# Low parts of projection and down weights, and the HGRN level products, moved from GpSimd to VectorE

## The chip, the cores and the metric

One Trainium2 chip, one core of it. The metric is device microseconds (us) of one execution of the whole program; a kernel's time is the median over runs. The engines go by the profile's names: PE is TensorE's matmul, PEld its weight load, DVE is VectorE, ACT is ScalarE, POOL is GpSimd, SP is SyncE, whose queue issues nearly all DMAs.

## What is computed

One layer (DEPTH = 1) of a hybrid streaming encoder on 1,152 tokens: 128 sample tokens (8 streams of 16) and 1,024 prompt tokens, D_MODEL = 1024, everything in float32.

```python
h = rmsnorm(x, norm1_w)
proj = einsum("btd,de->bte", h, w_in)                 # 3080 columns
xa, ga, z, xbc, dt, q, fpre, ig, og = split(proj, SPLIT_IDX)
ya = rglru(causal_conv(xa)) * gelu(ga)                # Griffin RG-LRU, 256 wide
yb = ssd_mixer(z, causal_conv(xbc), dt)               # Mamba-2 SSD, 512 wide
yc = hgrn_mixer(q, fpre, ig, og)                      # HGRN2, 256 wide
x = x + concat([ya, yb, yc]) @ w_out
h2 = rmsnorm(x, norm2_w)
x = x + (silu(h2 @ w_ffn_gate) * (h2 @ w_ffn_up)) @ w_ffn_down    # D_FF = 2816
y = rmsnorm(x, final_norm_w)

def hgrn_chunk(s, (q, lf, k, v)):                     # the part that the change touches
    bc = cumsum(lf, axis=1)
    decay = exp(where(causal, bc[:, :, None] - bc[:, None], -inf))
    att = einsum("bthk,bshk,btshk->bths", q, k, decay)
    o = einsum("bths,bshv->bthv", att, v) + einsum("bthk,bhkv->bthv", q * exp(bc), s)
```

The states of the three mixers are returned too.

## The kernel before

**High and low parts.** Matmuls of the projections and of the feed-forward part run three times each (`mm3`, lines 144 to 146): high by high, high by low and low by high part. A high part is the float32 value rounded to the engine's `fp32r` form, written by ScalarE with a Copy; the low part is the value less its high part, one `tensor_tensor` subtraction with both inputs in SBUF. `load_w` (line 152) does this for a weight tile of 128 x 1024: DMA into `wr_*`, Copy into `wh_*` (line 160), subtraction into `wl_*` (line 164). `split` (line 178) does the same for any tile (lines 179 and 180). Which engine subtracts is written out: in `load_w` every fourth weight tile of the projections, and one tile of `w_out`, goes to VectorE, the rest to GpSimd (`WV`, `WO`, `XV`, `XO`); of the third chunk of `w_out` the odd tiles go to VectorE too (`eng`).

**Stages.** Tokens stand in three chunks of 384. In order of time: the norm of the input and the first projection tiles `f0`, `f1`, `q0` (`pmf`, `pmq`); `proj_vdt` (tiles `ptv`, drained by lines 428 and 430 into `dtr` and `vs`) and `proj_og` (`ptog`); the HGRN mixer `mix_c`, nine token tiles of 128, among the RG-LRU projections (`pmxa`, `pmga`) and the eight `xbc` tiles (`pmb`, line 332); the gate projections (`ptz`); the SSD mixer `mix_b`, nine token tiles, with `w_out` (`pw`) between; the build of the feed-forward input; gate and up weights in pairs (`pS_*`, `pA_*`), some 460 us; then the down projection: five groups of weights after a first, each in two column sets of 320 and 256 columns a half, four output tiles `mp` and seven products of a Strassen scheme in each. VectorE adds each product from PSUM into SBUF (line 1204, `ac_*<-ac_*,pd`).

**HGRN levels.** For each token tile, `mix_c` goes through seven levels (four for the sample tile), two at a time in `W`. VectorE subtracts (lines 488 and 489), ScalarE takes the exponential (line 490), then the query half of `W` is multiplied by `q` into the block layout `qbd`, one instruction for each half of the partitions (line 498: half 0 on VectorE, half 1 on GpSimd), and the key half by `kk` in place (line 502, GpSimd). PE multiplies `W` by `qbd` into `pat` (line 139), and VectorE copies the masked result into `attc` (line 505).

**Down weights.** `prep_a` splits a tile of two rows of blocks: `split` of the first three quarters (768 wide; `mp` 3 on GpSimd, the others on VectorE), four combinations on VectorE (lines 1107 to 1110), `split` of all four combined blocks (1024 wide, line 1111, GpSimd). The result is `as`, and PE reads it one group later.

**What sets the order.** The tile framework puts instructions into each engine's queue in an order that it works out when the program is built, from priorities (program order, with raised priority inside `feed()` and around `mix_b`) and from its own timing of every instruction on its engine. The queues are then fixed: each engine runs its own in order and waits where an input is not there. So when an instruction changes engine, the order on all engines can change.

Of the kernel before, what the change touches and what calls it, by code (L numbers as in the profile page):

```python
# [16 lines left out]
ALU = mybir.AluOpType  # L17
# [34 lines left out]
WV = 4  # L52
# [12 lines left out]
WO = 0  # L65
XV = 100
XO = 1
# [23 lines left out]
def hybrid_step(ctx, tc, xT, xTp, vec, rows, nrow, wch, wtk0, wtk1, wout, wgate, wup, wdown,  # L91
# [59 lines left out]
    wcount, pcount, bcount = [0, 0], [0, 0], [0]  # L151

    def load_w(src, n, name, raw=None, ahead=True, eng=None):
        if raw is None:
            raw = wp.tile([P, 1056], F32, tag="wraw", name=f"wr_{name}", bufs=2)
        hi = wp.tile([P, 1056], F32R, tag="whi", name=f"wh_{name}")
        lo = wp.tile([P, 1056], F32R, tag="wlo", name=f"wl_{name}")
        with feed() if ahead else nullcontext():
            dma(raw[:, 0:n], src)
            S.activation(hi[:, 0:n], raw[:, 0:n], AF.Copy)  # L160
            o = name[0] == "o"
            wcount[o] += 1
            e = V if wcount[o] % (WV, XV)[o] == (WO, XO)[o] else G
            (eng or e).tensor_tensor(lo[:, 0:n], raw[:, 0:n], hi[:, 0:n].bitcast(F32), ALU.subtract)
        return hi, lo

# [299 lines left out]
    def halves(ap, m):  # L466
        v = ap.rearrange("p j (b two m) -> p (j b) two m", two=2, m=m)
        return v[:, :, 0, :], v[:, :, 1, :]

    def mix_c(t):  # L470
# [9 lines left out]
        for lg in range(l0, NLEV, 2):  # L480
            ls = range(lg, min(lg + 2, NLEV))
            W = pr.tile([P, 2, 2, P], F32, tag="W", name=f"W{t}_{lg}", bufs=2)
            for l in ls:
                m = 64 >> l
                b0, b1 = halves(bt, m)
                w0, w1 = halves(W[:, l - lg], m)
                mid = b0[:, :, m - 1:m].to_broadcast([P, P // m, m])
                V.tensor_tensor(w1, b1, mid, ALU.subtract)
                V.tensor_tensor(w0, mid, b0, ALU.subtract)
            S.activation(W[:, 0:len(ls)], W[:, 0:len(ls)], AF.Exp)  # L490

            Q = qbd[(lg // 2) % 2]
            pa = bank("b", f"pat{t}_{lg}", [2, 2, P])
            for l in ls:
                m = 64 >> l
                for r in range(2):
                    rs = slice(r * 64, r * 64 + 64)
                    (V, G)[r].tensor_tensor(Q[rs, l - lg, :, r, :].rearrange("p j (b m) -> p j b m", m=m),  # L498
                                    W[rs, l - lg].rearrange("p j (b two m) -> p j b two m", two=2, m=m)[:, :, :, 1],
                                    q[rs].rearrange("p j (b two m) -> p j b two m", two=2, m=m)[:, :, :, 1], ALU.mult)  # L500
                w0 = halves(W[:, l - lg], m)[0]
                G.tensor_tensor(w0, w0, halves(kk, m)[0], ALU.mult)
                for j in range(2):
                    mm(pa[:, l - lg, j, :], W[:, l - lg, j, :], Q[:, l - lg, j].rearrange("p r s -> p (r s)"))
                V.copy_predicated(
                    att.rearrange("p h (b two m) -> p h b two m", two=2, m=m)[:, :, :, 1, :],
                    lev[:, l, :].rearrange("p (b m) -> p b m", m=m).unsqueeze(1).to_broadcast([P, 4, 64 // m, m]),
                    pa[:, l - lg].rearrange("p j (r b m) -> p (j r) b m", r=2, m=m))
# [590 lines left out]
    def prep_a(g, mp):  # L1099
        t = stage(1024, f"wd{g}_{mp}")  # L1100
        v = a_view(mp)
        with feed():
# [5 lines left out]
            V.tensor_tensor(t[:, :, 3], t[:, :, 0], t[:, :, 3], ALU.subtract)  # L1108
            V.tensor_tensor(t[:, :, 0], t[:, :, 2], t[:, :, 0], ALU.subtract)
            V.tensor_tensor(t[:, :, 1], t[:, :, 1], t[:, :, 0], ALU.subtract)  # L1110
            split(v[:, 0, :, 3:7], v[:, 1, :, 3:7], t, G)


    acc = {}
# [281 lines left out]
```

## Time and profile before

| | us |
|---|---|
| median of 3 runs | 1501.31 (1500.36 to 1501.39) |
| profiled execution, whole | 1499.57 |
| its span, first to last instruction | 1497.8 |
| mean granted TensorE clock | 0.96 |
| PE busy | 1367.8 (91%) |
| DVE busy | 1122.1 (75%) |
| POOL busy | 792.9 (53%) |
| ACT busy | 513.9 (34%) |

The profiled execution is 1.77 us longer than its span and 1.74 us shorter than the median. A share of busy time is an average over stages with different limits. Of 40 equal slices of the span, those of the gate and up weights have PE busy throughout; in the others PE has gaps, and VectorE is then often the engine that is waited for.

### The profile page before, as it was taken

The page shows a single profiled execution, that of the slowest core. Times are in us where ns is not written, and L with a number is a line of the kernel's source. Part 1 is how long each engine was busy: PE and PEld are TensorE (multiplying, and loading weights), DVE is VectorE, ACT ScalarE, POOL GpSimd, SP SyncE. Part 2 cuts the span into 40 slices and gives each one's busy share as a digit, 9 for nine tenths or more (in the row PEclk, how much of TensorE's full clock was granted, in tenths as well). Part 3 has the DMA queues.
Part 4 walks back from the last instruction along what each step waited for, and adds up shares of the span by engine and source line. Part 5 has one row for each costly group of instructions (what it writes and reads, how often), then busy time and mean ns, then how long its engine had stood idle before and what let it go on. Part 6 is the DMA issues. An engine that isn't in the chain of part 4 may idle for free. (4 is left out here: it accounts for less than half of the span.)

```text
span 1497.8 us, 24592 instructions
## 1 busy us (share of the span) xinstructions
PE 1367.8 (91%) x9309; PEld 1315.9 (88%) x9309; DVE 1122.1 (75%) x2028; ACT 513.9 (34%) x839; POOL 792.9 (53%) x615
## 2 busy tenths in 40 slices
PE   7979988899997889878799999999999999988886
PEld 6979887799987778878699999999999989988876
DVE  8476799888758688599646675665666768989896
ACT  6413334333344134354322222232231443322322
POOL 5336487767345555433534554544555464475553
PEclk9989999899999899988899999999999999999988
DMA  7253221432366786841413222223322262543523
GB/s 249 75 173 102 71 68 50 104 96 75 100 224 238 225 285 208 273 167 37 150 55 112 100 96 99 70 84 113 112 98 99 85 218 85 171 149 92 172 64 127
DMA packets 103370, 193.67 MB, mean 129 GB/s; under 512 B 10380, under 2 KB 62676, under 8 KB 103124
## 3 DMA queue, kind: packets, MB, share of 16 engines
q1 hardware_dynamic: 98356, 184.24, 37.4%
q0 software_dynamic: 4896, 7.87, 1.9%
q8 instruction: 73, 1.20, 0.3%
q14 instruction: 45, 0.37, 0.1%
HBM read 136.83 MB, written 55.23 MB: 128 GB/s over the span
## 5 line engine op out<-in xcount | busy, mean ns | idle before, releaser
L144 PE MATMUL pd<-e,as 128*128 128x320 f32 (+1 forms) x560 | 170.2, 305 | 25.4 <-DVE ac_pt L1204 9.1
L145 PE MATMUL pd<-e,as 128*128 128x320 f32 (+1 forms) x560 | 166.4, 298 | 0.8 <-DVE e L1096 0.8
L146 PE MATMUL pd<-e,as 128*128 128x320 f32 (+1 forms) x560 | 163.3, 297 | 0.6 <-POOL as L180 0.6
L144 PEld LDWEIGHTS pd<-e,as 128*128 128x128 f32 x560 | 106.8, 191 | 32.1 <-DVE ac_pt L1204 9.4
L180 POOL TENSOR_TENSOR al_u<-wr_u,ah_u 128x1024 fp32r<-128x1024 f32 x30 | 72.1, 2404 | 118.4 <-ACT ah_u L179 118.4
L180 POOL TENSOR_TENSOR al_g<-wr_g,ah_g 128x1024 fp32r<-128x1024 f32 x30 | 72.3, 2412 | 88.6 <-ACT ah_g L179 88.0
L145 PEld LDWEIGHTS pd<-e,as 128*128 128x128 f32 x560 | 107.1, 191 | 1.2 <-DVE e L1096 1.1
L146 PEld LDWEIGHTS pd<-e,as 128*128 128x128 f32 x560 | 106.5, 192 | 0.9 <-POOL as L180 0.9
L1005 POOL TENSOR_TENSOR g<-g,pt_u 128x256 f32<-128x256 f32 (+1 forms) x80 | 77.3, 985 | 22.9 <-DVE pt_u L1004 16.1
L179 ACT ACTIVATE ah_g<-wr_g 128x1024 fp32r<-128x1024 f32 x30 | 31.7, 1060 | 146.6 <-PE pS_u L145 71.8
L144 PE MATMUL pw<-mT,wh_o 128*128 128x384 f32 x192 | 69.1, 363 | 11.4 <-DVE xr L785 5.5
L498 POOL TENSOR_TENSOR qbd<-W,qkb 64x128 f32<-64x128 f32 x60 | 51.7, 861 | 48.7 <-ACT W L490 16.0
L144 PE MATMUL pS_g<-b,ah_g 128*128 128x256 f32 (+1 forms) x240 | 71.3, 298 | 5.2 <-ACT ah_g L179 5.2
L146 PE MATMUL pA_g<-b,al_g 128*128 128x256 f32 (+1 forms) x240 | 71.2, 297 | 0.5 <-POOL al_g L180 0.5
L144 PE MATMUL pA_g<-b,ah_g 128*128 128x256 f32 (+1 forms) x240 | 71.4, 298 | 0.0
L145 PE MATMUL pA_g<-b,ah_g 128*128 128x256 f32 (+1 forms) x240 | 71.0, 296 | 0.0
L145 PE MATMUL pA_u<-b,ah_u 128*128 128x256 f32 (+1 forms) x240 | 71.0, 296 | 0.0
L145 PE MATMUL pS_g<-b,ah_g 128*128 128x256 f32 (+1 forms) x240 | 71.0, 296 | 0.0
L144 PE MATMUL pA_u<-b,ah_u 128*128 128x256 f32 (+1 forms) x240 | 70.9, 295 | 0.0
L146 PE MATMUL pA_u<-b,al_u 128*128 128x256 f32 (+1 forms) x240 | 70.8, 295 | 0.0
L144 PE MATMUL pS_u<-b,ah_u 128*128 128x256 f32 (+1 forms) x240 | 70.4, 295 | 0.0
L145 PE MATMUL pS_u<-b,ah_u 128*128 128x256 f32 (+1 forms) x240 | 70.3, 295 | 0.0
(722 smaller groups left out, 5118.2 us busy)
## 6 DMA issues: line engine op xcount, KB each, us to landing
wr_o<-in_dram SPq DMA_DIRECT2D x24, 512.0 KB, 5.3
wr_g<-in_dram SPq DMA_DIRECT2D x20, 512.0 KB, 3.5
wr_u<-in_dram SPq DMA_DIRECT2D x20, 512.0 KB, 3.6
wd<-in_dram SPq DMA_DIRECT2D x15, 512.0 KB, 3.7
wr_t<-in_dram SPq DMA_DIRECT2D x14, 512.0 KB, 3.8
fr<-ffd SPq DMA_DIRECT2D x11, 640.0 KB, 4.0
ffd<-g SPq DMA_DIRECT2D x10, 640.0 KB, 3.0
ffd<-g SPq DMA_DIRECT2D x10, 512.0 KB, 2.9
```

What stands on the lines that cost most here:

```text
L144: T.matmul(out, ah, bh, start=start, stop=False)
L145: T.matmul(out, ah, bl, start=False, stop=False)
L146: T.matmul(out, al, bh, start=False, stop=stop)
L179: S.activation(dst_hi, src, AF.Copy)
L180: eng.tensor_tensor(dst_lo, src, dst_hi.bitcast(F32), ALU.subtract)
L498: (V, G)[r].tensor_tensor(Q[rs, l - lg, :, r, :].rearrange("p j (b m) -> p j b m", m=m), W[rs, l - lg].rearrange("p j (b two m) -> p j b t ...
L1005: G.tensor_tensor(g, g, u, ALU.mult)
```

## The change

Three places put work on VectorE that GpSimd did:

- the subtraction in `load_w` always runs on VectorE (where `eng` is given it was VectorE already);
- in `mix_c` both halves of the query product (line 498) and the key product (line 502) run on VectorE;
- the second `split` of `prep_a` (line 1111) subtracts on VectorE.

Nothing is added to or taken from what is computed, and no DMA or matmul changes. GpSimd keeps its part of the gate and up weights, of the feed-forward inputs, of the first `split` for `mp` 3, of the SSD mixer and of the sums at the end.

```diff
@@ load_w
             o = name[0] == "o"
             wcount[o] += 1
-            e = V if wcount[o] % (WV, XV)[o] == (WO, XO)[o] else G
+            e = V
             (eng or e).tensor_tensor(lo[:, 0:n], raw[:, 0:n], hi[:, 0:n].bitcast(F32), ALU.subtract)
@@ mix_c
                 for r in range(2):
                     rs = slice(r * 64, r * 64 + 64)
-                    (V, G)[r].tensor_tensor(Q[rs, l - lg, :, r, :].rearrange("p j (b m) -> p j b m", m=m),
+                    V.tensor_tensor(Q[rs, l - lg, :, r, :].rearrange("p j (b m) -> p j b m", m=m),
...
                 w0 = halves(W[:, l - lg], m)[0]
-                G.tensor_tensor(w0, w0, halves(kk, m)[0], ALU.mult)
+                V.tensor_tensor(w0, w0, halves(kk, m)[0], ALU.mult)
@@ prep_a
-            split(v[:, 0, :, 3:7], v[:, 1, :, 3:7], t, G)
+            split(v[:, 0, :, 3:7], v[:, 1, :, 3:7], t, V)
```

The built order shows what the diff doesn't. Three places follow.

On DVE, where the projection `ptv` begins: `vs<-ptv_690` (with `dtr`) empties the first PSUM tile of that projection, the lines 410 are the running sums of the forget gates, and lines 311 empty the tiles of `q1`. Before:

```order
L405 SCALAR_TENSOR_TENSOR ct_547<-f_310,ct_547 128x1152
L405 SCALAR_TENSOR_TENSOR ct_548<-f_311,ct_548 128x1152
L410 SCALAR_TENSOR_TENSOR bc_558<-cm,ct_547 128x128
L410 SCALAR_TENSOR_TENSOR bc_558<-cio,ct_547 128x128 x8
L410 SCALAR_TENSOR_TENSOR bc_573<-cm,ct_548 128x128
L410 SCALAR_TENSOR_TENSOR bc_573<-cio,ct_548 128x128 x8
L428 SCALAR_TENSOR_TENSOR dtr<-ptv_690,rstd_86,rw 128x8
L430 TENSOR_SCALAR vs_715<-ptv_690,rstd_86 128x256
L311 SCALAR_TENSOR_TENSOR q_589<-pmq_0_596,rrow 128x384
```

After the change, at the same place on DVE:

```order
L405 SCALAR_TENSOR_TENSOR ct_547<-f_310,ct_547 128x1152
L164 TENSOR_TENSOR wl_t_953<-wr_t_951,wh_t_952 128x1024
L428 SCALAR_TENSOR_TENSOR dtr<-ptv_690,rstd_86,rw 128x8
L430 TENSOR_SCALAR vs_715<-ptv_690,rstd_86 128x256
L410 SCALAR_TENSOR_TENSOR bc_558<-cm,ct_547 128x128
L410 SCALAR_TENSOR_TENSOR bc_558<-cio,ct_547 128x128 x8
L405 SCALAR_TENSOR_TENSOR ct_548<-f_311,ct_548 128x1152
L428 SCALAR_TENSOR_TENSOR dtr<-ptv_748,rstd_86,rw 128x8
L410 SCALAR_TENSOR_TENSOR bc_573<-cm,ct_548 128x128
L311 SCALAR_TENSOR_TENSOR q_589<-pmq_0_596,rrow 128x384
```

The low part of a weight tile has come in, and the first `ptv` drain now stands ahead of all eighteen running sums instead of behind them; the `q1` drains stand ahead of the last eight.

On PE, in the first projection tiles: `prr_159` is the small matmul that spreads the first chunk's norm over the partitions. Before it stood between two `f` tiles:

```order
L144 MATMUL pmf_1_391<-hT_162,whi_f_97 128x384
L145 MATMUL pmf_1_391<-hT_162,whi_f_97 128x384
L146 MATMUL pmf_1_391<-hT_162,wlo_f_98 128x384
L139 MATMUL prr_159<-dg_155,cio 128x384
L145 MATMUL pmf_1_417<-hT_162,wh_f_131 128x384
```

After the change it stands inside the `q0` tile of the second chunk:

```order
L144 MATMUL pmq_1_443<-hT_162,wh_q_136 128x384
L145 MATMUL pmq_1_443<-hT_162,wh_q_136 128x384
L146 MATMUL pmq_1_443<-hT_162,wl_q_137 128x384
L139 MATMUL prr_159<-dg_155,cio 128x384
L144 MATMUL pmq_1_443<-hT_162,wh_q_136 128x384
```

It moved back by 32 matmuls (place 99 to place 131 in PE's queue).

On DVE, in the second group of down weights, column set 256: the lines 1204 empty PSUM, lines 1107 to 1110 combine weight blocks, and `as_11657<-wd_0` is the low part that came over. Before:

```order
L1204 TENSOR_TENSOR ac_pt_11689<-ac_pt_11689,pd_022_12451 128x256
L1109 TENSOR_TENSOR wd_1_12400<-wd_1_12400 128x2x128
L1204 TENSOR_TENSOR ac_g_11686<-ac_g_11686,pd_021_12459 128x256
L1204 TENSOR_TENSOR ac_pt_11690<-ac_pt_11690,pd_030_12476 128x256
L1110 TENSOR_TENSOR wd_1_12400<-wd_1_12400 128x2x128
```

After the change:

```order
L1204 TENSOR_TENSOR ac_pt_11689<-ac_pt_11689,pd_022_12451 128x256
L180 TENSOR_TENSOR as_11657<-wd_0_12333,as_11657 128x2x512
L1109 TENSOR_TENSOR wd_1_12400<-wd_1_12400 128x2x128
L1204 TENSOR_TENSOR ac_g_11686<-ac_g_11686,pd_021_12459 128x256
L1204 TENSOR_TENSOR ac_pt_11690<-ac_pt_11690,pd_030_12476 128x256
```

One long subtraction stands between two drains where there was none.

## Rows read from the trace of the kernel before

**Rows 1.** Page, part 1: busy us (share of the span), instructions.

```profile
PE 1367.8 (91%) x9309; PEld 1315.9 (88%) x9309; DVE 1122.1 (75%) x2028; ACT 513.9 (34%) x839; POOL 792.9 (53%) x615
```

**Rows 2.** Busy time by stretch: length, engines' busy us (instructions), PEclk, DMA share, GB/s.

```profile
100.00:300.00 200.00, 182.54 (x1157) 166.68 (x1156) 167.55 (x352) 75.40 (x130) 137.91 (x132) 0.94 0.28 82
...
400.00:650.00 250.00, 216.16 (x1340) 201.24 (x1338) 185.70 (x301) 97.99 (x186) 131.59 (x90) 0.94 0.72 232
...
1200.00:1450.00 250.00, 223.83 (x1599) 216.47 (x1597) 217.81 (x383) 80.73 (x101) 148.29 (x94) 0.97 0.44 139
```

**Rows 3.** PE's waits: who waited for whom, us in total, times, longest.

```profile
PE pat L139 <- POOL W L502: 10.3, 6, 4.5
PE ptv L144 <- DVE vs L430: 9.6, 1, 9.6
PE pd L144 <- DVE ac_pt L1204: 9.1, 5, 2.7
...
PE pmb L748 <- DVE ws L744: 4.0, 2, 2.5
...
PE prr L139 <- DVE dg L208: 2.1, 1, 2.1
```

**Rows 4.** Line 164 alone by stretch: length, busy us (instructions) of DVE, of POOL.

```profile
100.00:400.00 300.00, 4.88 (x4) 26.64 (x12) 0.95 0.28 83
400.00:650.00 250.00, 10.11 (x6) 66.39 (x27) 0.94 0.72 232
```

**Rows 5.** POOL's groups by line: busy us, mean ns | idle before, ended by.

```profile
L498 POOL TENSOR_TENSOR qbd<-W,qkb 64x128 f32<-64x128 f32 x60 | 51.7, 861 | 48.7 <-ACT W L490 16.0 <-DVE W L489 10.6 <-DVE attc L505 10.1
L502 POOL TENSOR_TENSOR W<-W,qkb 128x128 f32<-128x128 f32 x60 | 50.6, 845 | 4.6
...
L180 POOL TENSOR_TENSOR as<-wd,as 128x1024 fp32r<-128x1024 f32 x15 | 37.6, 2513 | 37.0 <-ACT as L179 37.0
...
L180 POOL TENSOR_TENSOR as<-rrow,as 128x1024 fp32r<-128x1024 f32 x5 | 12.3, 2470 | 12.1 <-ACT as L179 12.1
```

**Rows 6.** DVE's timeline, start and duration in us: a low part and small products, unhindered.

```profile
620.60 1.22 DVE L164 TENSOR_TENSOR wl_o<-wr_o,wh_o 128x1024 fp32r<-128x1024 f32 x1
621.74 0.55 DVE L219 TENSOR_TENSOR sq<-sq,tq 128x384 f32<-128x384 f32 x1
...
223.84 0.28 DVE L489 TENSOR_TENSOR W<-qkb 128x128 f32<-128x128 f32 x1
224.04 0.28 DVE L488 TENSOR_TENSOR W<-qkb 128x128 f32<-128x128 f32 x1
```

**Rows 7.** DVE's groups of the same two kinds by line, as in rows 5.

```profile
L498 DVE TENSOR_TENSOR qbd<-W,qkb 64x128 f32<-64x128 f32 x60 | 26.5, 469 | 0.8 <-ACT W L490 0.8
...
L164 DVE TENSOR_TENSOR wl_t<-wr_t,wh_t 128x1024 fp32r<-128x1024 f32 (+1 forms) x4 | 6.1, 1530 | 2.8 <-ACT wh_t L160 2.8
```

**Rows 8.** Timelines of DVE and POOL in the down stage.

```profile
1303.58 0.94 DVE L180 TENSOR_TENSOR as<-wd,as 128x768 fp32r<-128x768 f32 x1
...
1307.76 2.43 POOL L180 TENSOR_TENSOR as<-rrow,as 128x1024 fp32r<-128x1024 f32 x1 [6.38 <-ACT as L179]
...
1308.44 2.57 DVE L180 TENSOR_TENSOR as<-wd,as 128x768 fp32r<-128x768 f32 x1
...
1428.81 2.56 DVE L1109 TENSOR_TENSOR wd<-wd 128x256 f32<-128x256 f32 x1
```

**Rows 9.** Timelines of DVE and POOL around the SSD mixer and `w_out`.

```profile
549.09 5.75 DVE L744 SCALAR_TENSOR_TENSOR ws<-ws,ssb,nwr 128x256 f32<-128x256 f32 x2 [0.89 <-POOL ssb L172]
...
552.19 2.36 POOL L164 TENSOR_TENSOR wl_o<-wr_o,wh_o 128x1024 fp32r<-128x1024 f32 x1
```

**Rows 10.** DVE's timeline where the projection `ptv` begins.

```profile
74.77 7.10 DVE L410 TENSOR_TENSOR_SCAN bc<-cio,ct 128x128 f32<-128x128 f32 x8
...
84.75 0.47 DVE L430 TENSOR_SCALAR vs<-ptv,rstd 128x256 f32<-128x256 f32 x1
```

## The prediction

> **What bounds the kernel now.** I read the page first: VectorE is busy 1122.1 us and GpSimd 792.9 [rows 1], so by the averages VectorE, at 75%, is the busier of the two and gets more. An average hides where that matters, so the next view is busy time by stretch. In the gate and up stretch PE never stops and nothing of the change is there; the three stretches with most of the change have PE busy 182.54 of 200, 216.16 of 250 and 223.83 of 250 us [rows 2]. Only their gaps, some 77 us, and two gaps before 100 us can grow or shrink. Third, PE's waits say who ends them: in the mixer GpSimd's key products (`pat <- POOL W`, 10.3 us in all), in the first 100 us VectorE's drain of `ptv` (9.6) and `prr` (2.1), around `w_out` the scaling at line 744 (4.0), in the down stage the drains at line 1204 (the largest group 9.1) [rows 3]. So VectorE sets PE's gaps, and the question is whether it has more or less to do.
>
> Fourth, the timelines, for how long VectorE really needs. The same subtraction of 768 columns takes 0.94 us at 1303.58 and 2.57 us at 1308.44; in the second case a GpSimd subtraction had run since 1307.76, for 2.43 us, and VectorE finished after it [rows 8]. At 549.09 two scalings at line 744 take 5.75 us, across a GpSimd low part at 552.19 [rows 9]; line 1109 takes 2.56 us at 1428.81 [rows 8]. Instructions with two SBUF inputs on the two engines exclude each other. I counted VectorE instructions that ran longer than others of their shape while one of the low parts that are to move was on GpSimd: 47, from the running sums at 74.77 [rows 10] to line 1109 at 1428.81 [rows 8], with 83.5 us over their undisturbed durations. That time is hidden in VectorE's 1122.1.
>
> **The change, part by part.** *Low parts, 43 weight tiles and 20 down tiles.* GpSimd loses 2.4 to 2.5 us each (15 and 5 down tiles) [rows 5]. VectorE gains, from start to next start, 621.74 - 620.60 = 1.14 us each [rows 6], 63 x 1.14 = 71.8 us. It is relieved of 83.5 us, 1.33 each. But it can still be held by what GpSimd keeps: its present low parts average 1.53 us [rows 7], 0.31 over the 1.22 of the free one [rows 6]. With a third of GpSimd's work gone I take two thirds of that, 0.2. Net per low part 1.14 + 0.2 - 1.33 = 0.0 us: a wash in VectorE's load, between -0.19 (never held) and +1.45 (no relief at all). I take 0.0, since both sides come from counted instructions. What changes is the sort of waits: a planned 1.14 us in place of an unplanned 1.5 to 2.4 us that hits whatever drain comes next.
>
> *Level products, 60 query halves and 60 key products.* On GpSimd they take 861 and 845 ns [rows 5]. On VectorE a product of this size costs 224.04 - 223.84 = 0.20 us from start to start [rows 6], 120 x 0.20 = 24 us. The relief: VectorE's own halves average 469 ns [rows 7] where such a product takes 0.28 alone [rows 6], so 60 x 0.19 = 11 us. Net +13 us for the mixer, on 300 us in which the first 200 have VectorE busy 167.55 [rows 2]; it has room for that, but not everywhere. Against it stands latency: for two levels GpSimd's four products take 2 x (0.861 + 0.845) = 3.4 us in a row; six on VectorE take 1.2.
>
> The row gives such a product a duration of 0.28 us, with the next start after 0.20 [rows 6]. [...]
>
> *What PE gains or loses, stage by stage.* (1) First 100 us. The order of VectorE's queue puts the first `ptv` drain ahead of the eighteen running sums, which before ended just before the drain at 84.75 [rows 10]. But the later `ptv` tiles still need the `q1` drains, and those stand behind ten of the sums and GpSimd's two long products of that stage. I keep half of the wait of 9.6: -5 us (0 to -9). (2) `prr_159` moves 32 matmuls back, which covers its 2.1 us [rows 3]: -2 (0 to -2.1). (3) Mixer, 100 to 400 us. The 10.3 us of waits for GpSimd's `W` [rows 3] turn into waits for VectorE, which has +13 us. These two ends are -10 and +13; nothing in the trace puts it nearer to one, and I take 0. (4) 400 to 650 us, with 27 moved low parts on GpSimd [rows 4]. Load unchanged, but the 4.0 us of PE behind line 744 [rows 3] came from two low parts on GpSimd [rows 9] that are gone: 549.09's 5.75 us would be near 1. I take -3, between -9 (those 4.0, and 0.19 for each of 27 low parts that is never held) and +3 (held as today, 0.11 more each). (5) Down stage, 20 low parts. PE's waits for line 1204 follow such held instructions, as the 2.57 us at 1308.44. But the added 1.14 us stand in front of the same drains, and VectorE is at 217.81 of 250 [rows 2]. I take -2, between -9 (20 x 0.19, and half of the 9.1 of [rows 3]) and +6 (each of the 20 held for 0.31 us ahead of a drain). Where nothing moved, 740 to 1200 us, I take nothing: GpSimd's queue gets shorter ahead of it, and PE has no gaps there.
>
> Sum: -5 - 2 + 0 - 3 - 2 = -12 us. Against the profiled execution 1499.57 - 12 = 1487.6, and the median stands 1.74 above that execution: 1489.
>
> **The rivals.** *A, slower: VectorE waits in line for the high parts.* GpSimd could afford to wait for ScalarE's Copy: 37.0 us before 15 down tiles alone, 2.5 each [rows 5], because nobody was queued behind. On VectorE the drains are queued behind. What it pays today before its own weight tiles is 2.8 us for four, 0.7 each [rows 7]. At 63 x 0.7 = 44 us, and with half of that in places where PE has no free PSUM tile, 22 us come on top of 1489: 1511. It decides from 12 us of PE time, that is from about 0.4 us a low part, in the `w_out` and down stretches, where DMA and ScalarE's Copy come just in time. For it: seven tenths and more of VectorE's time is taken there. Against it: the built order has room between a Copy's source and its subtraction (in the piece of the down stage several instructions lie between).
>
> *B, no change: the waits move.* PE's order waits for PSUM tiles and weights in a chain; a gap closed at 75 us or 550 us reopens at the next. The load of VectorE is a wash by my own count but for +13 in the mixer; if that costs as much as the first 100 us give, and the rest comes to nothing, the time is 1499 to 1503.
>
> *C, faster still: the exclusion was the main cause of PE's gaps.* Then most of VectorE's 83.5 + 11 us come back to the drains and the better ends of (1), (4), (5) hold: -9 - 2 - 3 - 9 - 9 = -32, 1469. Against it: GpSimd still runs over 500 us, and the products it keeps hold VectorE as before.
>
> **How the numbers follow.** Forecast, 1478 to 1498: 0.47. C, and what lies between: 0.10. A: 0.27. B: 0.16. The range of 8 in 10 runs from 1474, some way into C, to 1512, A at its price. A measurement of this kernel tells 0.2%, 3 us, from no change: faster by more (forecast and C, of which a little falls inside) 0.55, within 0.17, slower 0.28.
>
> **What would show it.** Right: VectorE's total busy time hardly grows although it has 183 instructions more, and GpSimd's falls by some 250 us to about 540; subtractions of 768 columns in the down stage near 0.94 us and line 744 near 0.47; no wait of 9 us before `ptv`; `pat` waits for VectorE for less than 10 us; PE's waits at line 1204 a little lower. Wrong: VectorE's idle time before lines 164 and 180 well above 12 us, ended by ScalarE's Copy (A); PE's idle time in the mixer up by 10 us with `pat` or `pmb` behind VectorE (the +13 reached PE); single low parts on VectorE at 2 us and more (the exclusion stays, the relief was mis-sized).

## The result, and the profile after

The changed kernel takes 1462.72 us (median; 1460.63 to 1465.86), the kernel before beside it 1500.84 (1499.48 to 1501.39): a ratio of 0.975, interval 0.973 to 0.977, 38 us faster. The forecast was 1489, 12 us faster, with a range down to 1474. The direction was right; the gain is three times the forecast and lies outside the range, beyond even rival C (1469).

The profiled execution of the changed kernel took 1465.86 us, its span 1464.1. First the page, busy time by engine, which answers [rows 1]:

```profile
PE 1360.7 (93%) x9309; PEld 1311.8 (90%) x9309; DVE 1123.0 (77%) x2211; ACT 514.6 (35%) x839; POOL 531.0 (36%) x432
```

VectorE took over 183 instructions from GpSimd, whose busy time fell by 262 us, and is as busy as before: 1123.0 us against 1122.1. By the totals nothing happened to it. By stage something did. Busy time by stretch (columns as in [rows 2]), cut at the same places of PE's work in both kernels: SSD mixer with `w_out`, and the down stage. Before:

```profile
482.00:666.00 184.00, 158.41 (x843) 147.44 (x844) 142.59 (x215) 71.28 (x127) 94.91 (x68) 0.91 0.71 229
...
1186.00:1451.00 265.00, 238.20 (x1697) 230.87 (x1697) 231.67 (x408) 87.46 (x112) 153.89 (x99) 0.97 0.43 135
```

After:

```profile
477.00:648.00 171.00, 152.13 (x847) 143.34 (x846) 130.48 (x231) 65.53 (x118) 48.20 (x50) 0.95 0.74 242
...
1170.00:1416.00 246.00, 234.67 (x1696) 229.05 (x1696) 221.56 (x425) 88.72 (x112) 101.41 (x78) 0.99 0.48 147
```

The same matmuls take 13 and 19 us less, with VectorE 12 and 10 us less busy although it does 16 and 17 instructions more. Those two places give most of the gain. Not all of it is gaps: PE's own busy time for these matmuls is 6.3 and 3.5 us less, at a mean granted clock of 0.95 in place of 0.91 and of 0.99 in place of 0.97; its gaps are 6.7 and 15.5 us less. What VectorE got back is seen in the durations of instructions that the change doesn't touch: lines 744 and 1109 (shortest / median / longest, ns). Before:

```profile
L744 DVE SCALAR_TENSOR_TENSOR ws<-ws,ssb,nwr x8: 472/1538/3232, 453.3 to 584.3; 128x256 f32<-128x256 f32 x8
...
L1109 DVE TENSOR_TENSOR wd<-wd x15: 403/417/2558, 1197.0 to 1428.8; 128x256 f32<-128x256 f32 x15
```

After:

```profile
L744 DVE SCALAR_TENSOR_TENSOR ws<-ws,ssb,nwr x8: 471/479/1260, 448.9 to 571.9; 128x256 f32<-128x256 f32 x8
...
L1109 DVE TENSOR_TENSOR wd<-wd x15: 405/415/947, 1180.8 to 1400.0; 128x256 f32<-128x256 f32 x15
```

And what it pays, by groups (busy us, mean ns | idle before), the rows that answer [rows 5 to 7]:

```profile
L164 DVE TENSOR_TENSOR wl_o<-wr_o,wh_o 128x1024 fp32r<-128x1024 f32 x24 | 31.4, 1307 | 9.9 <-ACT wh_o L160 9.9
...
L180 DVE TENSOR_TENSOR as<-wd,as 128x1024 fp32r<-128x1024 f32 x15 | 18.8, 1261 | 0.0
L164 DVE TENSOR_TENSOR wl_t<-wr_t,wh_t 128x1024 fp32r<-128x1024 f32 x14 | 17.6, 1262 | 3.8 <-ACT wh_t L160 3.8
```

A low part takes 1.26 to 1.31 us, close to the 1.22 of the free one. VectorE waits 9.9 us for ScalarE's Copy in front of 24 `w_out` tiles and not at all in front of these 15 down tiles.

PE's waits, as in [rows 3]:

```profile
PE pat L139 <- DVE attc L505: 6.9, 2, 6.5
...
PE pd L144 <- ACT as L179: 4.8, 3, 2.1
...
PE ptv L144 <- DVE q L311: 3.7, 1, 3.7
...
PE pd L146 <- DVE as L180: 2.7, 4, 1.0
...
PE prr L139 <- DVE dg L208: 2.1, 1, 2.1
...
PE pmb L748 <- DVE wb L744: 0.8, 1, 0.8
PE pd L139 <- DVE attc L505: 0.8, 1, 0.8
...
PE pat L139 <- DVE W L502: 0.7, 2, 0.5
```

The 9.6 us before `ptv` are 3.7, the 10.3 behind GpSimd's `W` are 0.7 behind VectorE's (a single wait of 6.5 for the mask copy is new), line 744 went from 4.0 to nothing for `ws`. The wait before `prr` is there as it was.

The drains of the down stage tell most. This is the view of line 1204, before: a group's durations, and who waited for the line.

```profile
L1204 DVE TENSOR_TENSOR ac_whi<-ac_whi,pd x62: 472/474/489, 1216.7 to 1451.2; 128x320 f32<-128x320 f32 x62
...
  PE pd L144: 24.8, 22
```

After:

```profile
  PE pd L144: 2.9, 6
```

PE waited 24.8 us for these drains, of which [rows 3] show the largest of six groups, 9.1; now it waits 2.9. A part comes back elsewhere: in the list above PE now waits 7.5 us for weights of this stage (4.8 for ScalarE's Copy, 2.7 for low parts on VectorE), for which it waited 0.6 before. The drain itself, with one input in PSUM, was never held: 472 to 489 ns. It stood behind instructions that were.

### The profile page after: what moved, and what is told of

It reads as the page before. It is cut to its first block, busy times and chain, and to the rows that moved or that the text cites. A ratio compares the mean times of both kernels' runs of the same rounds, so it can differ in the third digit from the quotient of the medians.

```text
span 1464.1 us, 24464 instructions
## 1 busy us (share of the span) xinstructions
PE 1360.7 (93%) x9309; PEld 1311.8 (90%) x9309; DVE 1123.0 (77%) x2211; ACT 514.6 (35%) x839; POOL 531.0 (36%) x432
## 4 chain that ended last, share of the span: by engine, by line
PE 35%; DVE 13%; DMA 4%; issue 2%; ACT 1%; POOL 1%; SPq 0%; DVEq 0%; POOLq 0%; ACTq 0%
PE pS_g L144 3%; PE pS_u L144 3%; PE pS_g L146 3%; PE pS_u L145 3%; PE pS_g L145 3%; PE pS_u L146 3%; DVE as L180 2%; PE pA_u L144 2%; PE pA_u L146 2%; PE pA_u L145 2%; PE pA_g L145 2%; PE pA_g L144 2%; PE pA_g L146 2%; DMA fr<-ffd 2%; DVE ac_whi L1204 1%
## 5 line engine op out<-in xcount | busy, mean ns | idle before, releaser
L144 PE MATMUL pd<-e,as 128*128 128x256 f32 (+1 forms) x560 | 167.8, 302 | 9.1 <-ACT as L179 4.8
L146 PE MATMUL pd<-e,as 128*128 128x256 f32 (+1 forms) x560 | 162.8, 298 | 2.7 <-DVE as L180 2.7
L145 PE MATMUL pd<-e,as 128*128 128x256 f32 (+1 forms) x560 | 165.1, 296 | 0.0
L144 PE MATMUL pA_g<-b,ah_g 128*128 128x256 f32 (+1 forms) x240 | 70.8, 295 | 0.0
L146 PE MATMUL pA_u<-b,al_u 128*128 128x256 f32 (+1 forms) x240 | 70.8, 295 | 0.0
L144 PE MATMUL pS_u<-b,ah_u 128*128 128x256 f32 (+1 forms) x240 | 70.6, 295 | 0.0
L144 PE MATMUL pmb<-hT,wh_b 128*128 128x384 f32 x192 | 68.3, 356 | 2.5 <-DVE rawb L329 1.8
L146 PE MATMUL pS_u<-b,al_u 128*128 128x256 f32 (+1 forms) x240 | 70.5, 294 | 0.0
## 6 DMA issues: line engine op xcount, KB each, us to landing
wr_o<-in_dram SPq DMA_DIRECT2D x24, 512.0 KB, 4.7
wr_g<-in_dram SPq DMA_DIRECT2D x20, 512.0 KB, 3.5
wr_u<-in_dram SPq DMA_DIRECT2D x20, 512.0 KB, 3.6
wd<-in_dram SPq DMA_DIRECT2D x15, 512.0 KB, 4.0
wr_t<-in_dram SPq DMA_DIRECT2D x14, 512.0 KB, 3.7
ffd<-g SPq DMA_DIRECT2D x10, 512.0 KB, 2.9
```

Source lines behind the costliest of these rows:

```text
L144: T.matmul(out, ah, bh, start=start, stop=False)
L145: T.matmul(out, ah, bl, start=False, stop=False)
L146: T.matmul(out, al, bh, start=False, stop=stop)
```

## Stages of all runs

From each trace: the time from the start to PE's first `ptv` matmul, from there to the first gate matmul (`pS_g0a`), to the first product of the down stage, and to its last; and VectorE's busy time in two of the stages (overlaps counted once). All in us; the runs are told of below.

| run | start | ptv to gate | gate, up | down | VectorE, ptv to gate | VectorE, down |
|---|---|---|---|---|---|---|
| before | 69.8 | 603.7 | 514.3 | 296.3 | 480.9 | 258.8 |
| e17_null | 70.8 | 612.8 | 515.4 | 294.8 | 473.2 | 259.4 |
| e19_null2 | 69.0 | 611.6 | 511.4 | 295.4 | 477.4 | 258.0 |
| e14_wout | 70.1 | 592.7 | 511.1 | 294.1 | 473.9 | 258.0 |
| e1_weights | 70.0 | 588.0 | 511.8 | 292.7 | 466.3 | 257.4 |
| e2_levels | 69.8 | 620.3 | 511.9 | 295.8 | 503.2 | 258.4 |
| e3_down | 70.0 | 614.3 | 518.1 | 279.0 | 476.4 | 250.9 |
| e16_early | 69.7 | 606.1 | 515.4 | 289.4 | 479.3 | 249.1 |
| e6_no_levels | 70.0 | 584.6 | 512.8 | 276.0 | 466.2 | 248.6 |
| e8 (e6, more down) | 68.2 | 584.1 | 512.6 | 276.8 | 467.5 | 255.7 |
| **after** | 68.3 | 590.5 | 513.0 | 278.3 | 484.3 | 250.3 |
| e7_more_down | 67.7 | 590.9 | 513.6 | 277.2 | 483.1 | 257.6 |
| e18_queue | 67.7 | 590.4 | 512.0 | 279.8 | 487.0 | 249.2 |
| e4_tt | 70.2 | 617.3 | 516.2 | 303.7 | 530.0 | 271.3 |
| e10_vdummy | 73.2 | 621.2 | 513.5 | 305.1 | 534.0 | 274.3 |
| e5_copy | 73.2 | 682.8 | 512.1 | 324.6 | 522.8 | 256.6 |
| e11_down_tt | 68.5 | 594.5 | 514.6 | 303.4 | 484.4 | 280.3 |
| e12_down_v | 68.2 | 590.7 | 513.4 | 303.7 | 483.5 | 279.1 |
| e13_down_copy | 68.8 | 587.7 | 514.6 | 305.6 | 484.5 | 264.7 |
| e15_stage_dma | 67.8 | 585.9 | 513.7 | 295.2 | 483.7 | 252.4 |

Each row is one execution; e3's is the slowest of its five (1497.24 us, median 1485.10), e15's the fastest of its five (1478.51, median 1483.73). In the stretch from `ptv` to the gate, before, e3 and e16 run the same queues and differ by 11 us (603.7, 614.3, 606.1), after and six others (e7, e18, e11 to e13, e15), equal there but for a few places, by 9 (585.9 to 594.5). So below, means of such groups are compared there, and nothing under 10 us is read from a pair.

## Experiment 1: the three edits apart

One of the three edits is made in the kernel before, the others left out. e1_weights:

```diff
-            e = V if wcount[o] % (WV, XV)[o] == (WO, XO)[o] else G
+            e = V
```

> The kernel before with the first edit alone: all low parts of projection and w_out weights on VectorE. Theory H (a GpSimd instruction with two SBUF inputs holds VectorE's drains, and taking such instructions away gives the time back where they were): the start gives about 4 us and the stretch of the SSD mixer and w_out about 10, 1487 us, and PE's waits for line 744 become small. Theory O (the new order of the queues, not the engine, made the gain): no stage has to keep its gain when the rest of the change is missing; any time from 1475 to 1505. Theory S (the three edits need each other, GpSimd must become nearly empty): less than 5 us.

Measured: 1477.88 us, ratio 0.984 (0.980 to 0.988), some 9 us under H's 1487.

e2_levels:

```diff
-                    (V, G)[r].tensor_tensor(Q[rs, ...
+                    V.tensor_tensor(Q[rs, ...
...
-                G.tensor_tensor(w0, w0, halves(kk, m)[0], ALU.mult)
+                V.tensor_tensor(w0, w0, halves(kk, m)[0], ALU.mult)
```

> The kernel before with the second edit alone: the HGRN level products on VectorE. Theory H: the 120 products are short, so little was held; the mixer gets 13 us of VectorE's work more and 10 us of PE's waits for GpSimd less: 1496 to 1506. Theory O: a new order in the mixer can shift the stages behind it by up to 10 us in either direction. Theory S: nothing, 1498 to 1503.

Measured: 1511.65 us, ratio 1.006 (1.003 to 1.008): slower, and above the ranges of H and S.

e3_down:

```diff
-            split(v[:, 0, :, 3:7], v[:, 1, :, 3:7], t, G)
+            split(v[:, 0, :, 3:7], v[:, 1, :, 3:7], t, V)
```

> The kernel before with the third edit alone: the 20 second low parts of the down weights on VectorE. The queues up to the down stage are as before but for a few places. Theory H: the drains at line 1204 are no longer held, PE's waits for them fall from 25 us to about 5, and the time by 15 to 19: 1482 to 1486. Theory O: the order in the down stage hardly changes, so the gain stays below 5. Theory S: below 5 as well, since GpSimd still has its weight tiles.

Measured: 1485.10 us, ratio 0.989 (0.984 to 0.994).

The parts add up: -1.6%, +0.6% and -1.1% make -2.1%; the whole change gave -2.5%, within the intervals of the parts. S falls. The stage table puts e1's gain between `ptv` and the gate and e3's in the down stage (PE's wait for line 1204 falls to 4.1 us), as H says. e2 lost 17 us between `ptv` and the gate against before, or 12 against the mean of that group.

A later run split e1 once more. e14_wout:

```diff
-            e = V if wcount[o] % (WV, XV)[o] == (WO, XO)[o] else G
+            e = V if o or wcount[o] % WV == WO else G
```

> The kernel before with the low parts of the w_out tiles alone on VectorE (the projection tiles stay at every fourth). It divides the 24 us of the run with all weight tiles. Theory H by stage: the waits around w_out and line 744 go, 10 to 14 us, 1487 to 1491, and the start keeps its 9.6 us wait before ptv; the rest of the 24 us came from the projection tiles. If w_out has all: 1476 to 1481.

Measured: 1485.04 us, 0.990 (0.987 to 0.992). The `w_out` tiles give about two thirds of e1's gain.

## Experiment 2: is it a new order only?

Most of these edits reorder hundreds of instructions. Two null runs keep the load and change the order up to `w_out` (WO = 2, then WO = 1):

```diff
-WO = 0
+WO = 2
```

> The kernel before, where another one of every four projection weight tiles has its low part on VectorE (WO = 2 in place of 0): the same number of low parts on each engine, but a new order of all queues up to w_out. It measures what a new order by itself does. If the order is worth little: within 3 us of before. If it is worth as much as the run with the level products alone lost in stages that its edit doesn't touch (13 us around w_out): up to 12 us in either direction.

Measured: 1508.80 us, 1.006 (1.004 to 1.008).

> As the run with WO = 2, with WO = 1: the kernel before with yet another of every four projection weight tiles on VectorE, the same load in a new order. The run with WO = 2 was 0.6 per cent slower than before. If orders of equal load scatter by some 10 us: anything from 1490 to 1512. If that run was an exception: within 3 us of before.

Measured: 1500.32 us, 0.999 (0.997 to 1.001).

So in two tries an order of equal load moved this kernel by up to 9 us, and e2's loss of 8 us alone proves nothing about the products. The gains of e1 and the whole are beyond it. For the down stage, whose queues the null runs hardly touch, e11 below speaks: its queues are those of the changed kernel but for a few dozen of VectorE's and some hundred of PE's instructions, and it loses 25 us there. As the main cause O falls.

## Experiment 3: the same VectorE time, held or planned

Behind each of 61 moved low parts a useless multiplication of the used-up raw tile by itself; on GpSimd in e4_tt:

```diff
-            e = V
-            (eng or e).tensor_tensor(lo[:, 0:n], raw[:, 0:n], hi[:, 0:n].bitcast(F32), ALU.subtract)
+            e, dum = V, name[0] != "q" and not eng and wcount[o] % (WV, XV)[o] != (WO, XO)[o]
+            (eng or e).tensor_tensor(lo[:, 0:n], raw[:, 0:n], hi[:, 0:n].bitcast(F32), ALU.subtract); dum and G.tensor_tensor(raw[:, 0:n], raw[:, 0:n], raw[:, 0:n], ALU.mult)
...
-            split(v[:, 0, :, 3:7], v[:, 1, :, 3:7], t, V)
+            split(v[:, 0, :, 3:7], v[:, 1, :, 3:7], t, V); G.tensor_tensor(t, t, t, ALU.mult)
```

> The changed kernel, and behind each weight tile and each of the 20 down tiles whose low part came over, GpSimd multiplies the used-up raw tile by itself: an instruction of the same size with two SBUF inputs, whose result nobody reads. VectorE keeps all its work. Theory H: VectorE's drains are held again, about 60 times by up to 1.5 to 2.4 us, on top of the low parts that it now has itself; the time goes back to before or above: 1490 to 1520. Theory O: the time stays within 5 us of the changed kernel, 1458 to 1468.

Measured: 1524.60 us, 1.016 (1.012 to 1.020) of before. The page shows that VectorE, which has no instruction more than in the changed kernel, is busy 65 us longer:

```profile
PE 1375.5 (90%) x9309; PEld 1320.2 (87%) x9309; DVE 1187.6 (78%) x2211; ACT 514.5 (34%) x839; POOL 670.2 (44%) x493
```

In e10_vdummy the same lines have V in place of G.

> The changed kernel, and behind the same 61 low parts VectorE itself multiplies the used-up raw tile by itself, 61 x 1.1 = 67 us of work in VectorE's own queue, as much as the 65 us that VectorE's busy time grew by in the run with these multiplications on GpSimd. Theory L (a microsecond of VectorE is a microsecond, planned or held): about 1520, as there. Theory P (work that stands in VectorE's queue goes where PE isn't waiting, held time hits the drains): half of that or less, 1465 to 1495.

Measured: 1523.81 us, 1.016 (1.013 to 1.018). VectorE's 61 instructions more give the same time:

```profile
PE 1378.1 (90%) x9309; PEld 1326.0 (87%) x9309; DVE 1199.5 (79%) x2272; ACT 517.4 (34%) x839; POOL 547.4 (36%) x432
```

By this pair VectorE's own work costs PE as much as time in which it is held, against P; but in both the raw tiles are free later and the queues have new orders. And in e5_copy GpSimd copies the tile twice instead (`G.tensor_copy(raw[:, 0:n], raw[:, 0:n])`, twice; `t` likewise):

> As the run with the 61 multiplications of the used-up raw tiles on GpSimd (which took 1.9 to 2.0 us each and cost 61 us against the changed kernel), but GpSimd copies the raw tile onto itself twice instead: the same buffers are released late, the same queue on GpSimd, but each instruction has one SBUF input. Theory H (the exclusion needs two inputs on both engines): VectorE is not held by them, the time stays within 12 us of the changed kernel, 1460 to 1475. Theory R (the cost came from buffers that are released late, so that loads start late): 1490 to 1525 again, with VectorE's busy time near 1123 us. Theory A (any GpSimd instruction holds VectorE): 1490 to 1525, with VectorE's busy time 40 us and more above 1123.

Measured: 1603.80 us, 1.068 (1.063 to 1.072), the worst of all. It isn't VectorE's load alone, since VectorE is busy 45 us longer for 141 us. PE waits for `w_out` weights, for which it hardly waited in any other kernel here:

```profile
PE pw L144 <- ACT wh_o L160: 22.4, 6, 7.1
PE pw L146 <- DVE wl_o L164: 16.8, 12, 6.5
```

The copies start after the low part and take 1.0 to 1.3 us each, so a raw tile is free 2 to 2.5 us later. That alone doesn't explain it: e4's multiplications keep a raw tile some 2 us longer as well (1.9 to 2.1 us, medians), and there PE waits 1.0 us for weight tiles between `ptv` and the gate, here 44.5. The queues of e5 stand in an order of their own, so the cause of its 141 us stays open. In all three runs raw tiles are free later, so none of them is a clean price.

## Experiment 4: the same in the down stage, without late buffers

The added work reads the high part and writes an unused piece of SBUF, and nobody waits for it. In e11 the other queues stay nearly the same; in e12 and e13 some 200 of VectorE's thousand instructions from the gate on stand elsewhere. e11_down_tt (e12_down_v has V, e13_down_copy two `G.tensor_copy` in that place; E0 stands for a view of `E[0][:, 4480:5504]`):

```diff
-            split(v[:, 0, :, 3:7], v[:, 1, :, 3:7], t, V)
+            split(v[:, 0, :, 3:7], v[:, 1, :, 3:7], t, V); G.tensor_tensor(E0, v[:, 0, :, 3:7].bitcast(F32), v[:, 0, :, 3:7].bitcast(F32), ALU.mult)
```

> The changed kernel, and in the down stage, behind each of the 20 low parts that came over, a GpSimd multiplication of the same size with two SBUF inputs that reads the high part and writes an unused piece of SBUF. No buffer is released later by it and nobody waits for it; the queues of the other engines stay as they were but for a few places. Theory H (a GpSimd instruction with two inputs holds VectorE and so the drains): VectorE's busy time grows by 20 x 1.0 to 1.6 us in the down stage, and the time by half of that and more, 1474 to 1490, with PE's waits at line 1204 back near 20 us. Theory R (the gain came from buffers that are free earlier): no change, 1460 to 1466.

Measured: 1491.68 us, 0.995 (0.992 to 0.997) of before.

> The same 20 multiplications in the same place, but on VectorE: 20 x 1.14 = 23 us of planned work. Theory L (a microsecond of VectorE costs PE the same, planned or held): as much for each microsecond as with the multiplications on GpSimd, 1474 to 1488. Theory P (planned work falls where PE isn't waiting): a third of that or less, 1463 to 1470.

Measured: 1490.74 us, 0.993 (0.991 to 0.996).

> The same place again, with two GpSimd copies of one SBUF input (1.17 to 1.3 us each in the last run with copies) in place of the one multiplication: about as long on GpSimd. Theory H with two inputs as its condition: VectorE is held little (a fifth of the copies' time, as in the last run, some 8 us), the time stays at 1462 to 1470. If any GpSimd instruction held VectorE alike: 1474 to 1490. It also tells whether the 140 us of the run with copies on the raw tiles came from the late release of buffers: then nothing of it shows here.

Measured: 1494.03 us, 0.996 (0.994 to 0.998).

The added groups, e11 first, then e13 (POOL's groups in the down stage, columns as above):

```profile
L1111 POOL TENSOR_TENSOR e<-as 128x1024 fp32r<-128x1024 f32 x20 | 44.0, 2199 | 48.1 <-ACT as L179 47.8
```

```profile
L1111 POOL CAST e<-as 128x1024 fp32r<-128x1024 f32 x40 | 59.5, 1488 | 18.7 <-ACT as L179 18.4
```

Against the changed kernel's 278.3 and 250.3 us, e11's down stage is 25.1 us longer with VectorE busy 30.0 longer, e12's 25.4 with 28.8: in this stage a microsecond of VectorE is worth 0.84 to 0.88 us of PE, held or planned, and P falls. H's sign came only in part: PE's waits for line 1204 are 8.6 us in e11, not near 20, and another 10.1 us are waits for low parts on VectorE, against 2.7.

e13 breaks my condition that both engines need two inputs. In its timeline two GpSimd casts stand beside two VectorE instructions that take 0.41 and 1.22 us undisturbed:

```profile
1237.24 2.22 POOL L1111 CAST e<-as 128x1024 fp32r<-128x1024 f32 x2 [6.84 <-ACT as L179]
...
1237.53 1.03 DVE L1108 TENSOR_TENSOR wd<-wd 128x256 f32<-128x256 f32 x1
1238.48 2.06 DVE L180 TENSOR_TENSOR as<-wd,as 128x1024 fp32r<-128x1024 f32 x1
```

In all, one-input casts hold VectorE 14.4 us for 59.5 of GpSimd, about a third for each microsecond of what the multiplications do (30.0 for 44.0). At the same price that is 12 of e13's 27 us. But 19 of the 27 lie in the last group of weights: 11 are gaps, the longest a wait of 6.1 us for ScalarE's Copy of a weight tile, and 8 are PE's own time for the same matmuls, at a mean granted clock of 0.83 against 0.95. So e13's time is no price of a cast.

## Experiment 5: staging tiles in the down stage

Load alone doesn't carry the gain: in the down stage VectorE's busy time falls by 8.5 us (258.8 to 250.3), worth 7 us by experiment 4, and PE gains 18 (15 in gaps, 3 in its own busy time). Another thing changed there: SP's queue, which loads the next tile into a staging tile once its readers are done. Weights, feed-forward inputs (line 1090) and the residual (line 1237) take turns in these tiles. Waits of SP's queue in the down stage before:

```profile
SPq L1090 <- POOL as L180: 53.5, 11, 9.5
SPq L1237 <- POOL as L180: 35.3, 4, 10.2
```

After, the low part's share of them:

```profile
SPq L1090 <- DVE as L180: 23.4, 10, 6.9
```

Other readers stand in for a part of it: all of SP's waits at these two lines are 181 us before and 164 after.

e15_stage_dma gives the changed kernel such a delay back by a DMA that reads the tile:

```diff
-            split(v[:, 0, :, 3:7], v[:, 1, :, 3:7], t, V)
+            split(v[:, 0, :, 3:7], v[:, 1, :, 3:7], t, V); G.dma_start(scd, t.rearrange("p f q s -> p (f q s)"))
```

> The changed kernel, and each of the 20 down tiles is also written to an unused place in DRAM, by a DMA from GpSimd's queue that reads the staging tile after its combinations are made. No engine computes more; the staging tile is free some microseconds later, as in the kernel before, where SP's queue waited 88.8 us in all for GpSimd's low parts before it could load into such a tile. Theory R (the later half of the down stage's gain came from staging tiles that are free earlier): 8 to 12 us of the gain go, 1470 to 1478. Theory H alone (the drains that GpSimd held were all): 1460 to 1467.

Measured: 1483.73 us, 0.990 (0.987 to 0.993) of before, 1.5% over the changed kernel's ratio and more than R had named. SP waits 73 us for that DMA, where it waited 88.8 for GpSimd in the kernel before (in all 179 at these two lines):

```profile
SPq L1090 <- DMA scd<-wd: 32.8, 7, 6.6
SPq L1237 <- DMA scd<-wd: 25.9, 4, 8.9
...
SPq L1237 <- DMA scd<-rrow: 14.4, 2, 8.9
```

The down stage is 17 us longer, 14 of it in PE's gaps, with VectorE's load equal within 2.1 us (252.4 against 250.3). How a late tile reaches PE is seen in VectorE's wait for the Copy of the feed-forward inputs, in which all that stands behind it in the queue waits too; before, after and e15:

```profile
DVE e L1096 <- ACT e L1093: 15.7, 10, 3.2
...
DVE e L1096 <- ACT e L1093: 10.6, 6, 2.3
...
DVE e L1096 <- ACT e L1093: 22.8, 9, 6.5
```

PE's waits for the drains of line 1204 are 9.9 us in e15, against 2.9. The added DMA moves 10 MB more, but the loads of line 1090 hardly take longer (4.2 us from issue to landing against 4.0, medians).

e16_early tries the reverse in the kernel before: GpSimd subtracts from a second copy (E0), so that the staging tile is free early.

```diff
-            split(v[:, 0, :, 3:7], v[:, 1, :, 3:7], t, G)
+            S.activation(v[:, 0, :, 3:7], t, AF.Copy); S.activation(E0, t, AF.Copy); G.tensor_tensor(v[:, 1, :, 3:7], E0.bitcast(F32), v[:, 0, :, 3:7].bitcast(F32), ALU.subtract)
```

> The kernel before, GpSimd keeps the 20 second low parts of the down weights, but ScalarE copies the tile once more into an unused piece of SBUF and GpSimd subtracts from that copy, so that the staging tile is free as early as in the changed kernel, while VectorE is held as before. (The copy is rounded like the high part, so these low parts come out as zero; the time is that of the full work, with 20 ScalarE copies of 0.9 us more.) Theory R: 8 to 12 us faster than before, 1488 to 1493. Theory H alone: within 3 us of before, or slower by ScalarE's copies.

Measured: 1495.53 us, 0.998 (0.997 to 0.999). The down stage is 7 us shorter, but VectorE was also busy 9.7 us less, since GpSimd's subtractions (2.60 us each; 2.51 and 2.47 in the kernel before) fell elsewhere, and ScalarE has 19 us more. At experiment 4's price that lighter VectorE is worth 8 us, so nothing is seen of a gain from tiles that are free early; ScalarE's work may have taken it. It doesn't separate the two; it shows only that the same load on VectorE (249.1) isn't enough for 278 us.

## Experiment 6: GpSimd's queue, and a faster version

e18_queue puts a tiny GpSimd step behind the Copy of 42 weight tiles, into unused columns:

```diff
+ ...; dum and G.tensor_tensor(lo[:, n:n + 16], hi[:, 0:16].bitcast(F32), hi[:, 0:16].bitcast(F32), ALU.mult)
```

> The changed kernel, and behind each of 42 weight tiles (not the wider ptv ones) GpSimd multiplies 16 columns of the high part with themselves into unused columns of the low part's tile. That is too short to hold VectorE, and the raw tile isn't kept by it; but GpSimd's queue again stands still until ScalarE's Copy of a weight tile is there, as in the kernel before (37.1 us around w_out), with its steps of the SSD mixer behind. The other queues stay as they were but for a few places. Theory Q (SSD steps that stood behind GpSimd's waits made half or more of the gain around w_out): 1469 to 1478. Theory H (the held VectorE instructions made it): 1460 to 1467.

Measured: 1465.46 us, 0.977 (0.975 to 0.979), although GpSimd waits 43.6 us for Copies around `w_out` (37.1 before). VectorE's busy time didn't grow by the tiny steps (1121.0 us, against 1123.0 in the changed kernel). GpSimd's SSD steps behind such waits cost nothing that can be measured. Q falls.

Three kernels go another way than the change. e6_no_levels is the change without the hunk in `mix_c`:

> The changed kernel with the HGRN level products put back as they were before (query half 1 and the key product on GpSimd), low parts of weights and down tiles on VectorE. If the parts add up (1.6 per cent and 1.1 per cent gained by the low parts, 0.55 per cent lost by the level products alone): 1455 to 1462. If the products only cost time while GpSimd has weight tiles among them (then they were right in the changed kernel): 1463 to 1475.

Measured: 1461.34 us, 0.974 (0.971 to 0.976). e7_more_down is the change with two further edits, and e8_no_levels_more_down has them on e6:

```diff
-PA = (3,)
+PA = ()
...
-                        (G if q else V).tensor_tensor(
+                        V.tensor_tensor(
```

> The changed kernel, and in the down stage the last low parts that GpSimd has come to VectorE too (the first split of one weight tile in four, and the low parts of the second rows of feed-forward inputs). Theory H: what is left on GpSimd there still holds VectorE for 16 us; these go, against about 25 us of planned work more on an engine that is busy for 90 per cent: 1455 to 1468. Theory L (load counts): 1470 to 1490.

Measured: 1464.32 us, 0.976 (0.973 to 0.979).

> A try at a faster version: low parts of all projection and w_out weights and of all down tiles on VectorE, and the low parts of the feed-forward inputs in the down stage too, with the HGRN level products as they were before. The products on GpSimd were worth 6 us of span in one run and the additional low parts in the down stage cost nothing in another: 1455 to 1463. If the down stage is by now bound by PE itself, no change from the run without the level products, 1459 to 1464.

Measured: 1459.81 us, 0.975 (0.972 to 0.978). All three intervals hold the changed kernel's 0.975: no version beat it. The level products on VectorE cost about 4 us between `ptv` and the gate (590 against 584 to 588), too little to show in the ratios.

## Why the prediction was right or wrong

**What bounds the kernel.** Right as to the gaps: they follow VectorE in the three stretches, and 30 us of added VectorE time cost 25 us in the down stage. But that only the gaps can grow or shrink was wrong: PE's busy time for the same 9,309 matmuls fell from 1367.8 to 1360.7, 7.1 of the 33.7 us between the two spans.

**Net load per low part, 0.0 us.** This term failed, and its range with it. Means by groups of the stage table: from `ptv` to the gate VectorE's load fell from 478.9 (before, e3, e16) to 466.7 (e1, e6, e8), 12 us or 0.31 for each of the 39 weight tiles that lie there; in the down stage from 258.8 to 250.3, 0.43 for each of 20. My bound was -0.19. Two errors. I charged 0.2 us a low part for being held by what GpSimd keeps; at 1.26 to 1.31 against 1.22 it is 0.04 to 0.09. And the counted relief of 1.33 was too small: the two stages ask for about 1.14 + 0.09 + 0.31 = 1.5 and 1.14 + 0.04 + 0.43 = 1.6. The trace of before has it: counting every VectorE instruction that ran at least 0.1 us over the shortest of its line and shape beside one of the 63, it is 55 with 93 us, 1.5 each, in place of 47 with 83.5. That VectorE's total stayed at 1123 us, my first sign of being right, is luck: some -21 us for the low parts and +18 for the level products cancel, where I had 0 and +13.

**From load to PE time.** The larger error. For (4) and (5) I bounded PE's gain by the waits of one row each: the 4.0 of line 744, half of the 9.1 of one group of line 1204 [rows 3]. That line had six groups, 24.8 us together, and the view of that line gives them in one row; 21.9 of them went. Term (5) was -2 with an end at -9 (its parts add up to -8.4), and is -18 by this pair of executions (-17 by e3); the terms up to the gate, -5, -2, 0 and -3, are -14.7 by this pair, and -19 by the means of the groups (608.0 to 590.1, and 1.5 at the start; 3 less without e3's slow row). Most of the -12 was the order of the queues in the first 100 us (-5 and -2); held instructions, which made more of the gain, had -5 in it. The mechanism was told rightly, the size of its terms failed, and the 7.1 us of PE's own time had no term.

**The first 100 us.** Half of the 9.6 us was forecast, 5.9 of it went, by the mechanism told: the drain now stands ahead of the sums (VectorE's timeline after; compare [rows 10]).

```profile
72.12 1.22 DVE L164 TENSOR_TENSOR wl_t<-wr_t,wh_t 128x1024 fp32r<-128x1024 f32 x1
73.26 0.22 DVE L428 SCALAR_TENSOR_TENSOR dtr<-ptv,rstd,rw 128x8 f32<-128x8 f32 x1
73.39 0.48 DVE L430 TENSOR_SCALAR vs<-ptv,rstd 128x256 f32<-128x256 f32 x1
```

The -2 for `prr` was wrong: it stands 32 matmuls later and still waits 2.1 us.

**Level products, +13 us of load, 0 of time.** Nearly right: VectorE's load grows by 17 to 18 us (466.7 to 484) where I had +13, PE's time by about 4.

**Rival A** didn't come. VectorE does wait for Copies, 9.9 us before the `w_out` tiles and some 6 before the others, above the 12 us that I had named as its mark, but PE's gaps closed all the same: the mark was a bad one, since idle time of VectorE counts only where a drain stands behind it. What came of A is the 7.5 us that PE now waits for weights in the down stage. **Rival B** is excluded by the measured 38 us. **Rival C** was right in direction and, with the better ends of my own terms, at 1469 still 6 us short (its sum holds a -3 that is no term's better end; without it, it is 1472); my reason against it, that GpSimd goes on holding VectorE, was the 0.2 us that turned out 0.04 to 0.09.

**What stays open.** That GpSimd's instructions hold VectorE's, and that this time reaches PE, is shown; that it is all of the 38 us is not. VectorE's smaller load explains 7 of the down stage's 17 to 18 us; staging tiles that are free earlier can carry more (e15), but VectorE's wait through them is only 5 us shorter than before (15.7 to 10.6), and e16 didn't show the two apart. Between `ptv` and the gate the load explains about 7 of 18 to 22 us (12 us at 0.6, the price of e4 and e10 there, which late raw tiles may have raised: 27 for 46 and 31 for 50). Of these 18 to 22 us, 8 to 9 are PE's own busy time for the same matmuls (540 to 531 or 532), at a mean granted clock of 0.95 in place of 0.93, and 10 to 13 are gaps. Over the runs the clock there is mostly lower where PE's gaps are longer (0.89 with 118 us of gaps in e5, 0.95 with 54 in e8), so gaps and clock go together; which of the two moves the other isn't shown. Two other orders of equal load gave none of the gain, GpSimd's queue none that can be measured (e18), and SP's waits for raw tiles hardly changed between before and e1 (98 and 101 us). That remainder has no shown cause.

## What to carry to other kernels

When two engines hold each other, their busy times mislead: look for one shape with a short and a long duration (in the kernel before, 0.94 and 2.57 us for one subtraction on VectorE, 0.45 to 3.58 for the key products on GpSimd), add up the excess by the instruction that ran on the other engine, and expect the relief where that excess stands, stage by stage. Before bounding a gain by waits, add up all groups that wait for the line, not the largest. And ask of a slow instruction not only whom it holds but which buffer it keeps: a queue that loads into that buffer waits with it, as SP's did for GpSimd's low parts, 88.8 us in the down stage before.

## What the runs showed of the hardware

In e13 GpSimd's casts, with one SBUF input, held VectorE's two-input instructions as well (14.4 us of VectorE's busy time for 59.5 us of casts, and a low part of 2.06 us beside casts in place of 1.22). The drains of line 1204 with 320 columns, which have one SBUF input and one in PSUM, stayed at 472 to 489 ns in the kernel before and at 471 to 490 in e13. My condition in the expectations, two inputs on both sides, was too narrow.

PE's busy time is no constant of the program: between `ptv` and the gate the same matmuls took 540 us at a mean granted clock of 0.93 (before, e3, e16) and 532 us at 0.95 (after and the six others).
